# Layer 0's scores, sums, values and gate products in float32r, with the 16-token tile stacked by parts, and pairs of layer 1's small matmuls issued together

## The chip, the cores and the metric

The kernel runs on one core of a Trainium2 chip. The metric is device time of one execution in microseconds (us). The kernel before takes 1430.6 us, the median of three runs (1430.48 to 1431.33).

Five engines work in parallel and each executes its own instructions in order: TensorE (PE in the profile; its weight loads are listed apart as PEld), VectorE (DVE), ScalarE (ACT), GpSimd (POOL) and SyncE (SP), which here only issues DMAs.

## What is computed

The reference runs 272 tokens (16 learned meta tokens and 256 frames; the padding slots ahead of them are never computed) of width 2048 through two residual layers. Cut to what matters here:

```python
# layer 0: _even_mixer, one projection feeds both kinds of heads
log_a = log_sigmoid(gu @ w_gate2 + b_gate) / 16            # GLA gate, rank 16
scores = einsum('bcthk,bcshk->bchts', q_dec, k_inv)        # GLA, causal
o_intra = einsum('bchts,bcshv->bcthv', scores, v)
z = einsum('bhqd,bhkd->bhqk', qb, k)                       # stick-breaking, 8 heads of 128
ls = where(mask, log_sigmoid(-z), 0.0)
within = einsum('bhqnk,kl->bhqnl', ls, later_in_block)     # sums over later keys
w = where(mask, exp(log_sigmoid(z) + log_between), 0.0)
out = einsum('bhqk,bhkd->bhqd', w, v)
# layer 1: _odd_mixer, Mamba-2 SSD, 8 groups of 8 heads
y_diag = einsum('bctsgh,bcsghp->bctghp', l_mat * cb[..., None], xdt)
```

Each mixer is followed by an output projection, a residual add and a layer norm. Everything is float32. The kernel computes a float32 product either as a float32 matmul, or as three float32r matmuls on parts: an operand is split into a rounded high part and the rest, and hi·hi, lo·hi and hi·lo are accumulated.

## The kernel before

All 272 tokens are kept transposed, as columns; features lie on the 128 partitions. The program is a fixed list of units (`L0`, `L1`), each with one 128x2048 weight slice of 1 MB that SP loads into one of three buffers, that ACT rounds (`whi`, L146) and that DVE subtracts to get the rest (`wlo`, L147; in layer 1 POOL takes some). An input unit is 16 blocks of three float32r matmuls (`three`, L165 to L167) of a 128x128 weight block against 272 token columns; output units of layer 1 have 512 columns (L453 to L455). These are called the main stream below.

Between the blocks of a unit `tick()` advances a list of generators, which hold everything else: gates, scores, transposes, values, norms. `finish()` makes a unit wait in program order for the mixers that it needs. The order within each engine is then set by the framework's list scheduler, which works on the program's order, priorities and its own costs; so small matmuls end up as clusters between two matmuls of the main stream.

The tokens make three tiles: 0 to 127, 128 to 255 and the last 16. With attention causal, scores for the keys of the first tile need 272 query columns, those of the second 144, those of the last 16. In a layer-0 head the kernel before has:

- GLA gate (`gate_gla`, L494): a float32 matmul of `wg2` against `guT`, whose 128 rows hold four partial sums of the 16 rows of `gu`.
- Values to token order (`to_tokens`): PE transposes of `vraw`; the first token tile is split into `v0h`/`v0l`, the other two (`vt1`, `vt2`) stay float32.
- GLA values (`mix_gla`, L643 to L647): three float32r matmuls of 272 columns, one float32 of 144 columns, one float32 of 16 rows and 16 columns, for each of four value blocks.
- Stick-breaking (`mix_sb`): scores L705 to L707 in float32; the sums over later keys L724/L725 in float32r for the first tile and L726 to L730 in float32 for the others; values L742 to L746 as in GLA.

In layer 1, `x_path` transposes two feature blocks at a time (L1053, L1054) and `mix_ssd` computes 64-column pairs of heads with six float32 matmuls for each of four blocks j (L1100, L1102, L1104). PSUM has four `pj` buffers for the main stream, two `po` buffers for the small work and two `z` banks.

## Time and profile before

| | us |
|---|---|
| median of three runs | 1430.6 |
| the profiled execution | 1430.63 |
| its span, first to last instruction | 1428.9 |
| PE busy | 1408.6 |
| DVE busy | 980.7 |
| ACT busy | 762.7 |
| POOL busy | 334.0 |

The profiled execution is an ordinary one: it lies 0.03 us from the median, and 1.7 us of it lie outside the span. Matmul durations in a profile overlap, since PE is pipelined: three main matmuls of 0.29 us each start 0.12 us apart. What a matmul costs is therefore read here from the starts of a timeline (the time to the next start), not from durations. A float32 matmul of the program appears in the trace as two MATMULs and two LDWEIGHTS (so "x2" is one product); a float32r matmul and a transpose appear as one. The profile's names for shapes are rows*columns of the weight block, then the moving operand; all are printed as f32.

### The profile page before, as it was taken

The numbers are of one execution on the slowest core, as the hardware profiler recorded it, in microseconds if no ns is written. First come the engines' busy times: TensorE is split into PE (matmuls) and PEld (weight loads), VectorE is DVE, ScalarE is ACT, GpSimd is POOL, SyncE is SP. The second block draws the span as 40 slices with busy tenths as digits, with TensorE's granted clock in tenths as the row PEclk, the third lists the DMA queues.
The fourth block names the chain that finished last, engine by engine and source line by source line (L and its number), as shares of the span: only waits on it lengthen the run. The fifth ranks groups of instructions, "written<-read, shape, count | busy, mean of one in ns | idle before, by whom it ended". The sixth has DMA issues, their size and how long they took to land. (4 is left out here: it accounts for less than half of the span.)

```text
span 1428.9 us, 26055 instructions
## 1 busy us (share of the span) xinstructions
PE 1408.6 (99%) x10780; PEld 1337.7 (94%) x10780; DVE 980.7 (69%) x1522; ACT 762.7 (53%) x1133; POOL 334.0 (23%) x287
## 2 busy tenths in 40 slices
PE   9999999999999999999999999999999999999996
PEld 8999999999999999999999999899898998989985
DVE  6746574575565465447799989576876767767677
ACT  6545454354344544445587656565555555555651
POOL 0000100100101010004401535343432433434323
PEclk9999999999999999999999999999999999999998
DMA  8545444445454445444435554564554555445651
GB/s 318 181 151 173 153 153 172 167 159 177 148 178 148 148 148 192 148 148 144 150 132 216 193 199 166 207 225 167 206 178 166 207 181 220 153 172 179 207 207 59
DMA packets 37719, 249.83 MB, mean 175 GB/s; under 512 B 4256, under 2 KB 6112, under 8 KB 9184
## 3 DMA queue, kind: packets, MB, share of 16 engines
q1 hardware_dynamic: 37168, 247.77, 49.5%
q8 instruction: 84, 1.38, 0.4%
q10 hardware_dynamic: 432, 0.39, 0.1%
q14 instruction: 35, 0.29, 0.1%
HBM read 245.94 MB, written 2.20 MB: 174 GB/s over the span
## 5 line engine op out<-in xcount | busy, mean ns | idle before, releaser
L165 PE MATMUL pj<-xhi,whi 128*128 128x272 f32 (+4 forms) x2560 | 733.7, 287 | 1.8 <-DVE fix L845 1.5
L166 PE MATMUL pj<-xlo,whi 128*128 128x272 f32 (+4 forms) x2560 | 731.1, 286 | 0.1
L167 PE MATMUL pj<-xhi,wlo 128*128 128x272 f32 (+4 forms) x2560 | 730.2, 286 | 0.0
L147 DVE TENSOR_TENSOR wlo<-raw,whi 128x1024 fp32r<-128x1024 f32 (+2 forms) x405 | 508.9, 1260 | 280.7 <-ACT whi L146 278.3
L146 ACT ACTIVATE whi<-raw 128x1024 fp32r<-128x1024 f32 (+2 forms) x435 | 451.1, 1039 | 393.0 <-PE pj L166 324.8
L165 PEld LDWEIGHTS pj<-xhi,whi 128*128 128x128 f32 x2560 | 481.6, 188 | 5.1 <-DVE fix L845 1.9
L166 PEld LDWEIGHTS pj<-xlo,whi 128*128 128x128 f32 x2560 | 482.3, 188 | 2.1 <-issue 0.6
L167 PEld LDWEIGHTS pj<-xhi,wlo 128*128 128x128 f32 x2560 | 481.7, 188 | 0.5
L165 PE MATMUL pj<-mixh,whi 128*128 128x272 f32 x384 | 111.6, 292 | 0.0
L166 PE MATMUL pj<-mixl,whi 128*128 128x272 f32 x384 | 110.5, 288 | 0.0
L167 PE MATMUL pj<-mixh,wlo 128*128 128x272 f32 x384 | 110.2, 287 | 0.0
L147 POOL TENSOR_TENSOR wlo<-raw,whi 128x1024 fp32r<-128x1024 f32 x30 | 75.6, 2521 | 134.7 <-ACT whi L146 129.5
L453 PE MATMUL pj<-whi,yh 128*128 128x512 f32 (+1 forms) x244 | 97.3, 399 | 0.0
L454 PE MATMUL pj<-wlo,yh 128*128 128x512 f32 (+1 forms) x244 | 94.9, 389 | 0.0
L455 PE MATMUL pj<-whi,yl 128*128 128x512 f32 (+1 forms) x244 | 94.3, 386 | 0.0
L248 POOL TENSOR_TENSOR gr<-gr,gsc 128x1088 f32<-128x1088 f32 x6 | 15.4, 2572 | 307.0 <-ACT gsc L247 307.0
L165 PEld LDWEIGHTS pj<-mixh,whi 128*128 128x128 f32 x384 | 72.1, 188 | 0.5
L166 PEld LDWEIGHTS pj<-mixl,whi 128*128 128x128 f32 x384 | 72.3, 188 | 0.3
L167 PEld LDWEIGHTS pj<-mixh,wlo 128*128 128x128 f32 x384 | 72.3, 188 | 0.1
L462 DVE SCALAR_TENSOR_TENSOR acc<-pj,rr,acc 128x512 f32<-128x512 f32 (+1 forms) x65 | 47.4, 737 | 28.3 <-PE pj L455 28.2
L1108 POOL TENSOR_TENSOR yu<-yu,gz 128x256 f32<-128x256 f32 x32 | 44.9, 1408 | 82.2 <-DVE yu L1107 79.1
L455 PEld LDWEIGHTS pj<-whi,yl 128*128 128x128 f32 x244 | 45.9, 188 | 9.8
(309 smaller groups left out, 1497.8 us busy)
## 6 DMA issues: line engine op xcount, KB each, us to landing
raw<-in_wts SPq DMA_DIRECT2D x212, 1024.0 KB, 4.8
ebc<-edr SPq DMA_DIRECT2D x8, 1664.0 KB, 6.5
raw<-in_wts SPq DMA_DIRECT2D x9, 256.0 KB, 5.4
hacc<-in_xT SPq DMA_DIRECT2D x7, 272.0 KB, 5.4
early<-in_wts SPq DMA_DIRECT2D x2, 512.0 KB, 7.5
lg<-in_lnr SPq DMA_DIRECT2D x1, 1024.0 KB, 4.6
lb<-in_lnr SPq DMA_DIRECT2D x1, 1024.0 KB, 5.9
out_h<-acc SPq DMA_DIRECT2D x2, 512.0 KB, 2.6
```

The source lines that it names most:

```text
L146: self.nc.scalar.activation(hi, src, AF.Copy)
L147: eng.tensor_tensor(lo, src, hi.bitcast(F32), op=ALU.subtract)
L165: mm(ps, whi, xhi, start=first, stop=False)
L166: mm(ps, whi, xlo, start=False, stop=False)
L167: mm(ps, wlo, xhi, start=False, stop=last)
L248: mul(c, c, e, op=ALU.mult)
L453: mm(ps, yh[:, kk, tt], hi[:, k, :], start=kk == 0, stop=False)
L454: mm(ps, yh[:, kk, tt], lo[:, k, :], start=False, stop=False)
L455: mm(ps, yl[:, kk, tt], hi[:, k, :], start=False, stop=kk == 3)
L462: self.nc.vector.scalar_tensor_tensor(a, ps, r[:, t : t + 1], a, op0=ALU.mult, op1=ALU.add)
L1108: nc.gpsimd.tensor_tensor(u, u, z[:, j, :], op=ALU.mult)
```

## The change

In layer 0:

- Values of all three token tiles are float32r parts. `to_tokens` now handles two value blocks at a time and fills `vh`, `vl` for both 128-token tiles. The last 16 tokens are stacked by parts along the rows in `v2` (rows 0 to 15 hi, 32 to 47 lo, 64 to 79 hi) and meet `s2` with its parts stacked as hi, hi, lo: one float32r matmul with 80 rows gives all three products. `values` then issues three matmuls of 272 columns, three of 144 and one of 16 instead of the five above.
- Stick-breaking scores: q and k are split when they leave PSUM (`sb_parts`), and nine float32r matmuls replace three float32 ones. Sums: two of 272, two of 144 against `nL_r`, two of 144 against `nones_r`, and the last tile stacked in 48 rows (`sp2`, `nL2`) in two small matmuls.
- `parts_of` splits all 432 columns instead of 272 and copies the 16-token parts into the stack on DVE.
- Gate products: `add4`, one float32 matmul, sums the four partial sums of `gu`; `guS` (96 rows: hi, hi, lo) against `wg2r` (hi, lo, hi) is one float32r matmul. `wg2` has one buffer instead of two. The new constants are built at the start on DVE and POOL.

In layer 1 `x_path` emits all four blocks' transposes of a group together (the 16-row ones into a `z` bank), and `mix_ssd` emits the matmuls of two blocks j together. The units, their order, the weights and their DMAs stay.

```diff
--- before.py
+++ after.py
@@ -285,20 +285,32 @@
-        self.nones, self.nL, self.nL_r = [lp.tile([P, P], d, tag=n, name=n) for n, d in (("nones", F32), ("nL", F32), ("nL_r", F32R))]
+        self.nones_r, self.nL_r = [lp.tile([P, P], F32R, tag=n, name=n) for n in ("nones", "nL")]
+        nones, nL = [lp.tile([P, T], F32, tag="gs2", name=n, bufs=2)[:, :P] for n in ("nones_f", "nL_f")]
...
-        self.sel = lp.tile([P, P], F32, tag="sel", name="sel")
+        v2 = [lp.tile([80, 512], F32R, tag=f"v2{i}", name=f"v2{i}") for i in range(2)]
+        s2 = [lp.tile([80, 1, 16], F32R, tag=f"s2{i}", name=f"s2{i}") for i in range(2)]
+        self.v2, self.s2 = v2, s2
+        self.sp2, self.nL2 = [lp.tile([48, n, 16], F32R, tag=t, name=t) for n, t in ((2, "sp2"), (1, "nL2"))]
+        add4 = lp.tile([P, 432], F32, tag="ge", name="add4")[:, :P]
         for q in range(4):
-            nc.gpsimd.memset(self.sel[32 * q : 32 * q + 1, :], 1.0)
+            for r in range(4):
+                vec.tensor_copy(add4[32 * q : 32 * q + 32, 32 * r : 32 * r + 32], self.ident[32 * q : 32 * q + 32, 32 * q : 32 * q + 32])
...
@@ -335,7 +347,18 @@
         vec.tensor_copy(self.guT, ps[NS][:, :T])
-        vec.tensor_copy(self.nL_r, self.nL)
+        gs = self.po()
+        nc.tensor.matmul(gs[:, :T], add4, self.guT, start=True, stop=True)
+        act(self.guS[:64], gs[:64, :T], AF.Copy)
+        vec.tensor_tensor(self.guS[64:96], gs[:32, :T], self.guS[:32].bitcast(F32), op=ALU.subtract)
...
+        for a in v2 + [a.rearrange("p a b -> p (a b)") for a in s2 + [self.sp2, self.nL2]]:
+            vec.tensor_scalar(a, nones[: a.shape[0], 0:1].broadcast_to(a.shape), 0.0, None, op0=ALU.mult)
+        for q in (0, 32):
+            vec.tensor_copy(self.nL2[q : q + 16, 0, :], nL[:16, :16])
...
-            self.wg2 = self.lp.tile([P, 256], F32, tag="wg2", name=self.nm("wg2"), bufs=2)
+            self.wg2 = self.lp.tile([P, 256], F32, tag="wg2", name=self.nm("wg2"))
...
-        nc.tensor.matmul(ps[:, :T], self.sel, self.guT, start=True, stop=True)
+        nc.tensor.matmul(ps[:, :T], self.selx, self.guS, start=True, stop=True)
@@ -486,12 +509,15 @@
-        wg2 = self.wg2
+        wg2 = lp.tile([96, 256], F32R, tag="wg2r", name=self.nm("wg2r"))
+        act(wg2, self.wg2[:96], AF.Copy)
+        vec.tensor_tensor(wg2[32:64], self.wg2[:32], wg2[:32].bitcast(F32), op=ALU.subtract)
...
-            nc.tensor.matmul(ps[:, :T], wg2[:, j * P : (j + 1) * P], self.guT, start=True, stop=True)
+            nc.tensor.matmul(ps[:, :T], wg2[:, j * P : (j + 1) * P], self.guS, start=True, stop=True)
@@ -520,42 +546,66 @@
-    def parts_of(self, src):
-    def to_tokens(self, ps, v0h, v0l, vt1, vt2, j):
+    def parts_of(self, src, stack=None, rows=()):
+        n = src.shape[-1]
+        p = [self.lp.tile([P, 432], F32R, tag=t, name=self.nm(t), bufs=2)[:, :n] for t in ("s0h", "s0l")]
+        self.nc.scalar.activation(p[0], src, AF.Copy)
+        self.nc.vector.tensor_tensor(p[1], src, p[0].bitcast(F32), op=ALU.subtract)
+        for i, r in enumerate(rows):
+            a = stack[32 * i : 32 * i + 16]
+            b = p[r][:16, 0:16].rearrange("p (a b) -> p a b", a=1).broadcast_to([16, a.shape[1], 16])
+            self.nc.vector.tensor_copy(a, b)
+        return p
+    def to_tokens(self, raws, vh, vl, v2, j):
...
+        yield
+        pts = [self.po() for _ in raws]
+        for i, raw in enumerate(raws):
+            for t in range(2):
+                nc.tensor.transpose(pts[i][:, t * P : (t + 1) * P], raw[:, t * P : (t + 1) * P], self.ident)
+            nc.tensor.transpose(pts[0][:16, 256 + i * P : 256 + (i + 1) * P], raw[:, 256:272], self.ident)
...
+        w = slice(j * P, (j + len(raws)) * P)
+        t2 = pts[0][:16, 256 : 256 + len(raws) * P]
+        nc.scalar.activation(v2[:16, w], t2, AF.Copy)
+        for i, pt in enumerate(pts):
+            c = slice((j + i) * P, (j + i + 1) * P)
+            p = pt[:, : 2 * P].rearrange("p (t c) -> p t c", t=2)
+            nc.scalar.activation(vh[:, :, c], p, AF.Copy)
+            nc.vector.tensor_tensor(vl[:, :, c], p, vh[:, :, c].bitcast(F32), op=ALU.subtract)
+        nc.vector.tensor_tensor(v2[32:48, w], t2, v2[:16, w].bitcast(F32), op=ALU.subtract)
+        nc.vector.tensor_copy(v2[64:80, w], v2[:16, w])
...
+    def values(self, o, vh, vl, v2, c, sh, sl, s2):
+        mm = lambda r, a, b, start=False, stop=False: self.nc.tensor.matmul(
+            o[:, r], a, b, start=start, stop=stop, skip_group_check=True
+        )
+        for t, r, w in ((0, slice(0, T), slice(16, 288)), (1, slice(128, T), slice(288, 432))):
+            mm(r, vh[:, t, c], sh[:, w], start=t == 0)
+            mm(r, vh[:, t, c], sl[:, w])
+            mm(r, vl[:, t, c], sh[:, w])
+        mm(slice(256, T), v2[:, c], s2[:, 0, :], stop=True)
...
-        self.tasks["v", h, j] = self.push(self.to_tokens(ps, *self.cur["v", h], j))
+        raw = lp.tile([P, T], F32, tag="vraw", name=self.nm("vraw"), bufs=2)
+        self.nc.scalar.activation(raw, ps[:, :T], AF.Copy)
+        if j % 2:
+            self.tasks["v", h, j] = self.push(self.to_tokens([self.vraw, raw], *self.cur["v", h], j - 1))
+        self.vraw = raw
@@ -633,18 +683,14 @@
-        sh, sl = self.parts_of(s[:, 16:288])
+        st = self.s2[h % 2]
+        sh, sl = self.parts_of(s, st, (0, 0, 1))
...
+            self.values(o, *v, slice(j * P, (j + 1) * P), sh, sl, st)
@@ -675,40 +721,43 @@
+    def sb_parts(self, ps, tag, scale):
+        p = self.lp.tile([P, 2, T], F32R, tag=tag, name=self.nm(tag))
+        self.nc.scalar.activation(p[:, 0, :], ps[:, :T], AF.Copy, scale=scale)
+        self.nc.vector.scalar_tensor_tensor(
+            p[:, 1, :], ps[:, :T], scale, p[:, 0, :].bitcast(F32), op0=ALU.mult, op1=ALU.subtract
+        )
+        return p
...
-        self.cur["q"] = q
+        self.cur["q"] = self.sb_parts(ps, ("qe", "gq")[h % 2], SDH ** -0.5)
-        self.nc.vector.tensor_copy(self.cur["k"], ps[:, :T])
+        self.cur["k"] = self.sb_parts(ps, ("ke", "gk")[h % 2], 1.0)
...
     def mix_sb(self, h, q, k, v, tv):
-        mm(zb[:, 16:288], k[:, 0:128], q, start=True, stop=False, **gk)
-        mm(zb[:, 288:432], k[:, 128:256], q[:, 128:T], start=False, stop=False, **gk)
-        mm(zb[:16, 0:16], k[:, 256:T], q[:, 256:T], start=False, stop=False, **gk)
+        for a, b in ((0, 0), (0, 1), (1, 0)):
+            mm(zb[:, 16:288], k[:, a, 0:128], q[:, b, :], start=a == b, stop=False, **gk)
+        for a, b in ((0, 0), (0, 1), (1, 0)):
+            mm(zb[:, 288:432], k[:, a, 128:256], q[:, b, 128:T], start=False, stop=False, **gk)
+        for a, b in ((0, 0), (0, 1), (1, 0)):
+            mm(zb[:16, 0:16], k[:, a, 256:T], q[:, b, 256:T], start=False, stop=False, **gk)
...
+        sp = e = lp.tile([P, 432], F32, tag="ge", name=self.nm("sbe"))
@@ -718,16 +767,19 @@
-        sph, spl = self.parts_of(sp[:, 16:288])
-        mm(zb[:, 16:288], self.nL_r, sph, start=False, stop=False, **gk)
-        mm(zb[:, 16:288], self.nL_r, spl, start=False, stop=False, **gk)
-        mm(zb[:, 144:288], self.nones, sp[:, 288:432], start=False, stop=False, **gk)
-        mm(zb[:, 288:432], self.nL, sp[:, 288:432], start=False, stop=False, **gk)
-        mm(zb[:, 272:288], self.nones[:16, :], sp[:16, 0:16], start=False, stop=False, **gk)
-        mm(zb[:, 416:432], self.nones[:16, :], sp[:16, 0:16], start=False, stop=False, **gk)
-        mm(zb[:16, 0:16], self.nL[:16, :16], sp[:16, 0:16], start=False, stop=True, **gk)
+        sph, spl = self.parts_of(sp, self.sp2, (0, 1))
+        for s in (sph, spl):
+            mm(zb[:, 16:288], self.nL_r, s[:, 16:288], start=False, stop=False, **gk)
+        for s in (sph, spl):
+            mm(zb[:, 288:432], self.nL_r, s[:, 288:432], start=False, stop=False, **gk)
+        for s in (sph, spl):
+            mm(zb[:, 144:288], self.nones_r, s[:, 288:432], start=False, stop=False, **gk)
+        last = zb[:, 144:432].rearrange("p (a c) -> p a c", a=2)[:, :, 128:144]
+        mm(last, self.nones_r[:48, :], self.sp2, start=False, stop=False, **gk)
+        mm(zb[:16, 0:16], self.nL2[:, 0, :], self.sp2[:, 0, :], start=False, stop=True, **gk)
...
+        self.values(o, *v, slice(0, P), wh, wl, s2)
@@ -1045,23 +1094,31 @@
+        if j == 0:
+            return
+        pts = [self.po(), self.po()]
+        p2 = self.zbank()
+        for pt, jj in zip(pts, (0, 2)):
+            for i in range(2):
+                for t in range(2):
+                    nc.tensor.transpose(
+                        pt[:, t * 256 + i * P : t * 256 + (i + 1) * P], xt[:, jj + i, t * P : (t + 1) * P], self.ident
+                    )
+        for i in range(4):
+            nc.tensor.transpose(p2[:16, i * P : (i + 1) * P], xt[:, i, 256:T], self.ident)
...
+        for pt, jj in zip(pts, (0, 2)):
+            h0 = g * HPG + 2 * jj
+            c = slice(jj * P, jj * P + 256)
+            for t in range(2):
+                d = bd(self.est[:, 1, t, h0 : h0 + 4]).broadcast_to([P, 4, 64])
+                vec.tensor_tensor(hv(xd[:, t, c]), hv(pt[:, t * 256 : (t + 1) * 256]), d, op=ALU.mult)
+        d = bd(self.est2[:, 1, g * HPG : (g + 1) * HPG]).broadcast_to([16, HPG, 64])
+        vec.tensor_tensor(hv(xd2[:, :]), hv(p2[:16, :]), d, op=ALU.mult)
@@ -1091,18 +1148,21 @@
-            o = self.po()
...
-                mm(r[i][:, 0:S], xd[:, 0, c[i]], M[:, h[i], 0:256], start=True, stop=False, **gk)
...
-            yield
+            if j % 2 == 0:
+                os = {jj: self.po() for jj in (j, j + 1)}
+                gk = dict(skip_group_check=True)
+                for jj, o in os.items():
...
+                        mm(r[i][:, 0:S], xd[:, 0, c[i]], M[:, h[i], 0:256], start=True, stop=False, **gk)
...
+                yield
+            o = os[j]
```

Three places in the programs, as they were built. First PE, at the sums of a stick-breaking head (`z` is the bank with the scores, `s0h`/`s0l` the parts, `sp` the stack); before:

```order
L166 MATMUL pj_5113<-xlo,whi_5028 128x272
L725 MATMUL z_65<-s0l_5106,nL_r 128x272
L726 MATMUL z_65<-ppad,nones 128x144
L727 MATMUL z_65<-ppad,nL 128x144
L728 MATMUL z_65<-ppad,nones 128x16
L729 MATMUL z_65<-ppad,nones 128x16
L730 MATMUL z_65<-ppad,nL 16x16
L167 MATMUL pj_5113<-xhi,wlo_5029 128x272
```

and with the change:

```order
L165 MATMUL pj_5201<-xhi,whi_5154 128x272
L774 MATMUL z_65<-s0l_5191,nL 128x272
L776 MATMUL z_65<-s0h_5190,nL 128x144
L776 MATMUL z_65<-s0l_5191,nL 128x144
L778 MATMUL z_65<-s0h_5190,nones 128x144
L778 MATMUL z_65<-s0l_5191,nones 128x144
L781 MATMUL z_65<-sp_151,nones 128x2x16
L782 MATMUL z_65<-sp_151,nL_152 16x16
L166 MATMUL pj_5201<-xlo,whi_5154 128x272
```

One float32 product of 144 columns each for `nones` and `nL` has become two float32r ones, and the three products with the 16-token tile have become two with 48 rows. The cluster stands, as before, between two matmuls of the main stream.

Second PE, in `mix_ssd` of a late group (`M` is the decay matrix, `xd` the tokens-first x); before:

```order
L455 MATMUL pj_13229<-whi_13169,yl_11375 128x512
L1100 MATMUL po_13255<-M_12684,xd_12729 64x256 x2
L1102 MATMUL po_13255<-M_12684,xd_12729 64x144 x2
L1104 MATMUL po_13255<-mt,xd_1616_12730 64x16 x2
L453 MATMUL pj_13228<-whi_13197,yh_11374 128x512
L454 MATMUL pj_13228<-wlo_13198,yh_11374 128x512
L455 MATMUL pj_13228<-whi_13197,yl_11375 128x512
```

and with the change:

```order
L478 MATMUL pj_12480<-whi_12420,yl_10632 128x512
L1159 MATMUL po_12506<-M_11938,xd_11983 64x256 x2
L1161 MATMUL po_12506<-M_11938,xd_11983 64x144 x2
L1163 MATMUL po_12506<-mt,xd_1474_11984 64x16 x2
L1159 MATMUL po_12507<-M_11938,xd_11983 64x256 x2
L1161 MATMUL po_12507<-M_11938,xd_11983 64x144 x2
L1163 MATMUL po_12507<-mt,xd_1474_11984 64x16 x2
L476 MATMUL pj_12479<-whi_12448,yh_10631 128x512
```

Two blocks' matmuls now follow each other with no main matmul between them. This holds for fifteen of the sixteen pairs; in the first group the before kernel already has one such pair, and the first pair of the changed one is cut in two. The transposes of `x_path` are written together too, but in the built program each group still has two separate clusters of four 128-token and two 16-token transposes.

Third DVE, at the very start (`xlo` is the low part of the first tokens); before:

```order
L223 CAST ones_r<-ones 128x128
L338 CAST nL_r<-nL 128x128
L306 TENSOR_TENSOR xlo<-hacc,xhi 128x272
L147 TENSOR_TENSOR wlo_161<-raw_106,whi_160 128x256
L306 TENSOR_TENSOR xlo<-hacc,xhi 128x272
```

and with the change:

```order
L223 CAST ones_r<-ones 128x128
L356 CAST nones<-nones_f 128x128
L359 TENSOR_SCALAR v_147<-nones_f 80x512
L359 TENSOR_SCALAR v_148<-nones_f 80x512
L359 TENSOR_SCALAR s_149<-nones_f 80x16
L311 COPY add_153<-ident 32x32 x16
L355 CAST selx<-selx_f 96x128
L357 CAST nL<-nL_f 128x128
L359 TENSOR_SCALAR s_150<-nones_f 80x16
L359 TENSOR_SCALAR sp_151<-nones_f 48x32
L359 TENSOR_SCALAR nL_152<-nones_f 48x16
L318 TENSOR_TENSOR xlo<-hacc,xhi 128x272
```

The zeroing of the stacks and the sixteen copies that build `add4` now stand ahead of the first `xlo`.

More of the change, by code (lines that the diff above doesn't have):

```diff
@@ L617, in mix_gla @@
         q, k = self.cur["q", h], self.cur["k", h]
[L618 removed]
+        v = self.cur["v", h]
         g = self.cur["r", h]
[L620 removed]
+        yield from _wait(self.tasks["r", h], *[self.tasks["v", h, j] for j in (1, 3)])
         zb = self.zbank()
```

116 lines of the change are left out of this document (35 added, 81 removed).

## The prediction, made before the changed kernel was run

> **What bounds the kernel now.** I read the page first, then busy time by stretches (start:end and length in us, then busy us and instructions of PE, PEld, DVE, ACT, POOL, granted clock, DMA share, GB/s), then PE's waits.
>
> ```profile
> span 1428.9 us, 26055 instructions
> PE 1408.6 (99%) x10780; PEld 1337.7 (94%) x10780; DVE 980.7 (69%) x1522; ACT 762.7 (53%) x1133; POOL 334.0 (23%) x287
> ...
> 30.00:425.00 395.00, 395.00 (x3145) 389.84 (x3144) 243.95 (x398) 188.48 (x282) 26.25 (x28) 1.00 0.48 164
> 425.00:700.00 275.00, 275.00 (x2184) 269.74 (x2183) 157.56 (x203) 135.58 (x204) 49.43 (x77) 1.00 0.45 152
> 830.00:1417.00 587.00, 584.89 (x4237) 533.09 (x4236) 432.12 (x642) 324.98 (x457) 222.97 (x144) 1.00 0.52 183
> ...
> PE po L1053 <- POOL xt L955: 3.1, 5, 1.2
> ```
>
> From 30 to 700 us, layer 0, PE never stops, at the full granted clock; DVE is busy 60% of it and the DMA queues under half. In layer 1 the one wait of weight is 3.1 us for POOL ahead of the transposes. So a microsecond of PE time saved in layer 0 should be a microsecond of the end, as long as the other engines keep ahead. What each piece costs PE I read from starts on PE's timeline (start us, duration, line, tile, weights*shape, count).
>
> **The prices.** Ahead of each piece stands a main matmul, behind it another; from their starts I subtract the main stream's own 0.124 us each (601.20 − 601.08). Scores of one stick-breaking head:
>
> ```profile
> 601.08 0.29 PE L167 MATMUL pj<-xhi,wlo 128*128 128x272 f32 x1
> 601.20 0.62 PE L705 MATMUL z<-sqk 128*128 128x272 f32 x2
> 601.66 0.41 PE L706 MATMUL z<-sqk 128*128 128x144 f32 x2
> 602.00 0.21 PE L707 MATMUL z<-sqk 128*16 128x16 f32 x2
> ...
> 602.37 0.29 PE L166 MATMUL pj<-xlo,whi 128*128 128x272 f32 x1
> ```
>
> The piece costs 602.37 − 601.08 − 0.25 = 1.04 us. A float32 product of 272 columns takes 0.46, nearly four times the float32r 0.124. Sums of one head, with the values of one GLA block below them:
>
> ```profile
> 609.51 0.28 PE L166 MATMUL pj<-xlo,whi 128*128 128x272 f32 x1
> ...
> 609.76 0.41 PE L726 MATMUL z<-ppad,nones 128*128 128x144 f32 x2
> 610.00 0.41 PE L727 MATMUL z<-ppad,nL 128*128 128x144 f32 x2
> 610.34 0.39 PE L728 MATMUL z<-ppad,nones 16*128 16x16 f32 x2
> 610.58 0.37 PE L729 MATMUL z<-ppad,nones 16*128 16x16 f32 x2
> 610.88 0.21 PE L730 MATMUL z<-ppad,nL 16*16 16x16 f32 x2
> ...
> 611.25 0.29 PE L165 MATMUL pj<-xhi,whi 128*128 128x272 f32 x1
> ```
>
> ```profile
> 99.26 0.28 PE L165 MATMUL pj<-xhi,whi 128*128 128x272 f32 x1
> ...
> 99.76 0.41 PE L646 MATMUL po<-spad,gvt 128*128 128x144 f32 x2
> 100.09 0.39 PE L647 MATMUL po<-spad,gvt 16*128 16x16 f32 x2
> ...
> 100.64 0.29 PE L167 MATMUL pj<-xhi,wlo 128*128 128x272 f32 x1
> ```
>
> Sums: 611.25 − 609.51 − 0.25 = 1.49, and 0.13 for L724, which stands apart: 1.62. Values: 1.38 − 0.25 = 1.13. A float32 product of 144 columns takes 0.24 (609.76 to 610.00), and 0.34 where a matmul with fewer rows follows (610.00 to 610.34): 0.10 for the change of shape. L728 streams only 16 columns and yet takes 0.24, 0.12 for each of its two halves: below some 130 columns the load of 128 weight columns sets the pace.
>
> **The open price** is that of a float32r matmul of 144 columns; this trace has none under 256. Lower bound: its share of columns, 144/272 of 0.124 = 0.066. Upper bound: it is run as a float32 product, 0.24. I take 0.12, the weight load, because each of these matmuls loads 128 weight columns and L728 pays that with next to no columns. The small products of 16 columns I take at 0.03 to 0.07 with few weight columns (L730's two halves and the next load together take 0.14) and 0.12 with 128.
>
> The Trainium skill, "TensorE: Matmul & The Clock Gate", section "Back-to-back issue gap", gives about 81 ns per matmul of 128 columns in a sustained stream; by it the 120 new matmuls of 144 columns would cost some 4 us less than below. The same sentence has 131 ns for 512 columns, where this trace's main rows already have 124 ns for 272, so the trace does not bear it out.
>
> **Part by part.** Sum against the profiled execution's 1430.63 us, which is the median within 0.03.
>
> - Scores, 8 heads: 3 x 0.124 + 2 x 0.12 + 0.07 + 0.17 (three 16-column products and the next load) = 0.85 for 1.04: 1.5 us gained.
> - Sums, 8 heads: 0.25 + 4 x 0.12 + 0.15 (the two stacked products and the next load) = 0.88, and 0.17 for two changes of shape, since 48 rows are again fewer than 128: 1.05 for 1.62, 4.6 us. Without that change of shape 1.4 us more.
> - Values, 16 GLA blocks and 8 heads (there L742 to L746 are the same five products): 0.375 + 3 x 0.12 + 0.12 = 0.855 for 1.13: 24 x 0.275 = 6.6 us. I count no change of shape for 80 rows; at 0.17 each it would take 4.1 us back.
> - Gate products:
>
> ```profile
> 30.40 0.29 PE L167 MATMUL pj<-xhi,wlo 128*128 128x272 f32 x1
> 30.53 0.62 PE L356 MATMUL po<-guT,sel 128*128 128x272 f32 x2
> 30.98 0.62 PE L494 MATMUL po<-guT,wg 128*128 128x272 f32 x2
> ...
> 31.57 0.29 PE L166 MATMUL pj<-xlo,whi 128*128 128x272 f32 x1
> ```
>
> L356 and eight L494 cost 0.46 each; nine float32r at 0.125 and one new float32 (`add4`) replace them: 9 x 0.335 − 0.46 = 2.55 us.
> - Layer 1's pairs. One block, and two blocks that already stand together in group 0:
>
> ```profile
> 1261.36 0.39 PE L454 MATMUL pj<-wlo,yh 128*128 128x512 f32 x1
> 1261.58 0.39 PE L455 MATMUL pj<-whi,yl 128*128 128x512 f32 x1
> 1261.90 0.65 PE L1100 MATMUL po<-M,xd 128*64 128x256 f32 x4
> ...
> 1262.95 0.50 PE L453 MATMUL pj<-whi,yh 128*128 128x512 f32 x1
> 1263.29 0.40 PE L454 MATMUL pj<-wlo,yh 128*128 128x512 f32 x1
> ```
>
> ```profile
> 804.32 0.28 PE L166 MATMUL pj<-xlo,whi 128*128 128x272 f32 x1
> 804.53 0.65 PE L1100 MATMUL po<-M,xd 128*64 128x256 f32 x4
> ...
> 805.58 0.65 PE L1100 MATMUL po<-M,xd 128*64 128x256 f32 x4
> ...
> 806.86 0.29 PE L165 MATMUL pj<-xhi,whi 128*128 128x272 f32 x1
> ```
>
> Main matmuls of 512 columns start 0.22 to 0.23 apart (1261.58 − 1261.36). Alone: 1263.29 − 1261.58 = 1.71, less two of them, 0.45: 1.26. Together: 2.54 − 0.25 = 2.29. So 0.23 a pair; 14 new pairs: 3.2 us. The second block's matmuls now fill the other `po` buffer, so the next pair waits until DVE has read both; the built order has 18 main matmuls (4 us) between pairs, and I cost it at nothing.
> - Transposes: in the built order the clusters of `x_path` stay two per group, and most of `to_tokens` stay single. Fewer alternations of 128 and 16 columns: 0.5 us (0 to 1). POOL's 3.1 us stay; the first cluster stands later, the second earlier.
> - The start loses. DVE sits idle 1.84 us ahead of its first `xlo`; about 3 us now go in front of it: two zeroings of 512 columns, some 0.5 each, and sixteen copies, 0.07 apart if they go like the small copies below, plus a few casts.
>
> ```profile
> 4.39 0.44 DVE L306 TENSOR_TENSOR xlo<-hacc,xhi 128x272 fp32r<-128x272 f32 x1 [1.84 <-ACT xhi L305]
> ...
> 714.70 0.15 DVE L844 COPY uv<-po 64x2 f32<-64x2 f32 x1
> 714.77 0.14 DVE L844 COPY uv<-pj 128x2 f32<-128x2 f32 x1
> ...
> L590 DVE SCALAR_TENSOR_TENSOR gq<-pj,qe 128x16 f32<-128x16 f32 x8 | 1.3, 165 | 0.0
> ```
>
> PE's L166 waits behind it; I take 1.0 us (0.3 to 2.2, the last if a copy takes L590's 0.165).
> - DVE's added work in layer 0 is costed at nothing, hidden by the 40% of DVE that is idle: per stick-breaking head one more split from PSUM (0.44), two splits of 432 instead of 272 columns, five stack copies (0.165 each) and a wider value split, together about 1.9 us; per GLA head about 2.1. Eight and four of them: 23 us over 670 us. Uncovered it costs up to these 23 us. SP's `wg2` loads now wait for ACT and DVE to read the one buffer, with weight loads queued behind; three buffered units of 6 us each cover that.
>
> Sum: 1.5 + 4.6 + 6.6 + 2.55 + 3.2 + 0.5 − 1.0 = 17.95 us. 1430.63 − 17.95 = **1412.7 us**.
>
> **The rivals.**
>
> *B: under 256 columns float32r is no faster than float32.* For it: the kernel has not one such matmul today. Against it: nothing in the rows from 256 to 512 columns hints at a step. With 0.24 for each 144-column matmul the scores become 1.27 (1.8 us lost), the sums 1.53 (0.7 gained), the values 1.215 (2.0 lost); with the rest, 2.2 us are left: 1428.4. The skill's "FP8 and Floating Point Precision", "TensorE Precision Notes", has true FP32 as four passes and the reduced form as a read truncated to FP22, with no limit on columns; that speaks against B, and the 0.46 against 0.124 above agrees with four passes to one.
>
> *C: slower, through DVE.* The place is DVE's queue in layer 0: splits of weights (L147) stand behind the added copies, PE's next block behind the split. If all of the added 23 us reached PE, 1412.7 + 23 = 1436. It decides from the point where more than 18 of them do. Against it: PE today waits for no split from 30 to 700 us.
>
> *D: cheaper still.* Weight loads overlap, 144 columns cost 0.066 and the stack pays no change of shape: 120 x 0.054 + 1.4 = 7.9 us more: 1404.8.
>
> **How the numbers follow.** Forecast 0.68 (own range 1408 to 1418: the start, 80 and 96 rows, transposes), D 0.12, B 0.14, C 0.06. The range 1404 to 1422 leaves out B and C, 0.20. What can be told from no change is about 0.2%, 2.9 us: the forecast and D are faster (0.80); B lies at the edge, 0.03 faster, 0.09 the same, 0.02 slower; C 0.01 the same, 0.05 slower. So 0.83, 0.10, 0.07.
>
> **What would show it.** On PE's timeline: float32r matmuls of 144 columns 0.12 apart (B: 0.24, D: 0.07); a head's sums near 1.05 us, scores and values near 0.85; gates at 0.125; pairs in layer 1 near 2.3. PE still without waits from 30 to 700 us; if not, the wait names DVE and C is right. DVE's first `xlo` near 5.5 us. The forecast is wrong if PE's time per piece falls and the span does not.

## The result, and the profile after

The changed kernel takes **1409.91 us** (median of 4 runs, 1409.64 to 1410.04) where the kernel before took 1430.54 (4 runs, 1430.23 to 1431.33): ratio 0.9855, 95% interval 0.9838 to 0.9872. That is 20.6 us faster; 1412.7 was forecast, in a range of 1404 to 1422. The profiled execution took 1410.01 us, span 1408.3 against 1428.9.

Busy time by stretches of the changed kernel (same columns as in the prediction):

```profile
30.00:425.00 395.00, 395.00 (x3199) 393.24 (x3198) 255.28 (x417) 194.79 (x283) 29.73 (x29) 1.00 0.49 167
425.00:700.00 275.00, 272.50 (x2205) 269.67 (x2204) 176.54 (x269) 141.89 (x223) 51.58 (x77) 1.00 0.46 158
...
830.00:1396.50 566.50, 566.50 (x4107) 520.94 (x4108) 419.39 (x614) 315.20 (x441) 209.92 (x142) 1.00 0.52 183
```

PE still never stops from 30 to 425 us, at the full clock; DVE went from 244 to 255 us of these 395 and has room left. The second row now reaches past layer 0's norm (at 689 us, before at 703) and holds its waits; the third ends, like the one before, 12 us ahead of the end. PE's waits after (who waits and for whom: us in total, times, longest):

```profile
PE pj L165 <- ACT mixh L801: 1.0, 1, 1.0
...
PE po L1105 <- POOL xt L1004: 0.3, 1, 0.3
```

The 3.1 us for POOL's `xt` at the transposes fell to 0.3, and a wait of 1.0 us for ACT's `mixh` is new.

One head's sums on PE's timeline (start us, duration, line, tile, weights*shape, count):

```profile
446.13 0.29 PE L165 MATMUL pj<-xhi,whi 128*128 128x272 f32 x1
...
446.38 0.23 PE L776 MATMUL z<-s0h,nL 128*128 128x144 f32 x1
446.45 0.28 PE L776 MATMUL z<-s0l,nL 128*128 128x144 f32 x1
446.56 0.27 PE L778 MATMUL z<-s0h,nones 128*128 128x144 f32 x1
446.68 0.27 PE L778 MATMUL z<-s0l,nones 128*128 128x144 f32 x1
446.88 0.28 PE L781 MATMUL z<-sp,nones 48*128 48x32 f32 x1
447.01 0.17 PE L782 MATMUL z<-sp,nL 48*16 48x16 f32 x1
447.11 0.40 PE L166 MATMUL pj<-xlo,whi 128*128 128x272 f32 x1
447.34 0.29 PE L167 MATMUL pj<-xhi,wlo 128*128 128x272 f32 x1
```

447.34 − 446.13 − 2 x 0.124 = 0.96, and 0.13 for the first product, which stands apart: 1.10 for 1.62 before. Of the 144-column products the first costs 0.07 and each further one 0.11; ahead of the product on 48 rows stand 0.20. The last products of a block of values, with the weight loads (PEld) between them:

```profile
452.80 0.23 PE L590 MATMUL po<-s0h,gvh 128*128 128x144 f32 x1
452.80 0.19 PEld L590 LDWEIGHTS po<-s0l,gvh 128*128 128x128 f32 x1
452.87 0.27 PE L590 MATMUL po<-s0l,gvh 128*128 128x144 f32 x1
452.91 0.19 PEld L590 LDWEIGHTS po<-s0h,gvl 128*128 128x128 f32 x1
452.98 0.28 PE L590 MATMUL po<-s0h,gvl 128*128 128x144 f32 x1
453.02 0.19 PEld L590 LDWEIGHTS po<-s,v 80*128 80x128 f32 x1
453.09 0.22 PE L590 MATMUL po<-s,v 80*128 80x16 f32 x1
453.16 0.37 PE L166 MATMUL pj<-xlo,whi 128*128 128x272 f32 x1
```

Loads start no closer than 0.11 us (452.80, 452.91, 453.02), and the products follow them. On 80 rows nothing stands ahead of the stack.

The ledger over the whole trace: for every piece between main matmuls, the time from the main matmul ahead to the fourth one behind (fewer where the next piece comes sooner), less the main stream's own spacing, summed by kind. The 9,660 main matmuls are the same in both.

| us on PE | before | after | gained | forecast |
|---|---|---|---|---|
| scores (8) | 8.41 | 6.64 | 1.77 | 1.5 |
| sums (8) | 13.00 | 8.81 | 4.19 | 4.6 |
| values (24) | 27.42 | 20.99 | 6.43 | 6.6 |
| gate products | 4.16 | 1.62 | 2.54 | 2.55 |
| layer 1's M products (32 blocks) | 40.08 | 37.65 | 2.43 | 3.2 |
| x transposes | 15.69 | 11.22 | 4.47 | 0.5, with the next row |
| token transposes, norms | 9.06 | 9.07 | 0.0 | |
| layer 1's `cb` and sums of squares | 13.01 | 11.78 | 1.23 | 0 |
| start: to the first main matmul, and delays to 13 us | 6.83 | 7.61 | −0.78 | −1.0 |
| delays in the main stream after 13 us | 2.49 | 3.88 | −1.39 | 0 |
| behind the last matmul's start | 11.42 | 11.71 | −0.29 | 0 |

With 0.03 in pieces that the change leaves alone this is 20.6 us.

### The profile page after: what moved, and what is told of

Its sections match the earlier page's. It is cut to its first block, busy times and chain, and to the rows that moved or that the text cites. A ratio compares the mean times of both kernels' runs of the same rounds, so it can differ in the third digit from the quotient of the medians.

```text
span 1408.3 us, 26132 instructions
## 1 busy us (share of the span) xinstructions
PE 1390.1 (99%) x10765; PEld 1332.7 (95%) x10765; DVE 1003.8 (71%) x1613; ACT 769.3 (55%) x1138; POOL 320.9 (23%) x285
## 4 chain that ended last, share of the span: by engine, by line
PE 89%; DVE 6%; ACT 2%; issue 1%; DMA 1%; POOL 0%; ACTq 0%; SPq 0%; DVEq 0%; POOLq 0%
PE pj L165 23%; PE pj L166 23%; PE pj L167 23%; PE pj L476 4%; PE pj L478 4%; PE pj L477 4%; DVE wlo L147 2%; PE po L1159 1%; PE po L590 1%; ACT whi L146 1%; DVE xlo L816 1%; PE po L1161 1%; PE po L1163 0%; ACT hacc L923 0%; DMA ebc<-edr 0%
## 5 line engine op out<-in xcount | busy, mean ns | idle before, releaser
L166 PE MATMUL pj<-xlo,whi 128*128 128x272 f32 (+4 forms) x2560 | 731.7, 286 | 0.2 <-DVE xlo L318 0.2
L166 PEld LDWEIGHTS pj<-xlo,whi 128*128 128x128 f32 x2560 | 483.0, 189 | 1.8 <-issue 0.6
L166 PE MATMUL pj<-mixl,whi 128*128 128x272 f32 x384 | 110.4, 288 | 0.0
L166 PEld LDWEIGHTS pj<-mixl,whi 128*128 128x128 f32 x384 | 72.3, 188 | 0.2
L476 PEld LDWEIGHTS pj<-whi,yh 128*128 128x128 f32 x244 | 45.8, 188 | 9.0
```

What stands on the lines that cost most here:

```text
L166: mm(ps, whi, xlo, start=False, stop=False)
L476: mm(ps, yh[:, kk, tt], hi[:, k, :], start=kk == 0, stop=False)
```

## The experiments

Two theories at the start. **A**: the surplus over the forecast comes from layer 1's merges themselves, because the transposes no longer wait for POOL. **Rival**: the waits vanished because layer 0 now ends at another moment. Beside it stood the prices of the stack and of the small products, the start, and how much DVE work fits.

### The two halves apart, and x_path alone

E1 is the kernel before with `x_path` and `mix_ssd` of the change, E2 the changed kernel with these two as before. `mix_ssd` in E1:

```diff
-            o = self.po()
...
+            if j % 2 == 0:
+                os = {jj: self.po() for jj in (j, j + 1)}
...
+            o = os[j]
```

> The kernel before with only the merged clusters of layer 1 (x_path and mix_ssd of the change); layer 0 as before. Theory A (layer 1's part of the gain, 6.8 us between the end of layer 0 and the end of the span by the starts on PE, comes from the merges themselves: 3.2 us for 14 pairs, the rest because PE no longer waits for POOL at the transposes): 1430.5 - 6.8 = 1423.7 us, and PE's wait at the transposes for xt falls from 3.1 us to under 1. Rival (the waits for POOL vanished because layer 0 now hands over at another moment; the merges bring the pairs alone, as I predicted): 1430.5 - 3.2 = 1427.3 us, waits near 3 us.

> The changed kernel with x_path and mix_ssd of the kernel before: layer 0's changes alone. Theory A: 1409.9 + 6.8 = 1416.7 us, with waits for POOL's xt near 3 us again. Rival: 1409.9 + 3.2 = 1413.1 us, waits under 1. If the two parts are independent, this run's gain and that of the other half add up to 20.6 us.

E1: 1424.85 us, ratio 0.9957 (0.9940 to 0.9973), 6.1 us below the 1430.98 of the kernel before on the same chip. E2: 1415.25, ratio 0.9891 (0.9877 to 0.9906), 15.7 us below. Together 21.8 for 20.6: nearly independent. In E1 the transposes cost 10.69 us on PE and no wait for `xt` is left; in E2 they cost 14.57 and `PE po L1102 <- POOL xt L1004` stands at 2.3 us. Both times lie between the two forecasts, nearer to A's (off by 1.2 and 1.5 of the 3.6 us between them), and the waits go as A has it. Why shows in one group of the kernel before and of the changed one (POOL's row first, then PE's):

```profile
1060.20 1.37 POOL L955 TENSOR_TENSOR xt<-xt,xcl 128x544 f32<-128x544 f32 x1 [1.25 <-ACT xcl L954]
...
1061.26 0.28 PE L167 MATMUL pj<-xhi,wlo 128*128 128x256 f32 x1
1061.62 0.44 PE L1053 MATMUL po<-ident,xt 128*128 128x128 f32 x2
```

```profile
1042.02 1.38 POOL L1004 TENSOR_TENSOR xt<-xt,xcl 128x544 f32<-128x544 f32 x1 [1.26 <-ACT xcl L1003]
...
1047.16 0.28 PE L167 MATMUL pj<-xhi,wlo 128*128 128x256 f32 x1
1047.28 0.60 PE L1105 MATMUL po<-ident,xt 128*128 128x128 f32 x4
```

Before, the group's first cluster stood right behind POOL's multiplication (1061.57, then 1061.62), 0.24 us late. That is one of the mild cases: of the five waits that make up the 3.1 us, four, 2.8 us together, stand at the first cluster of a group, the longest 1.2 us. After, the first cluster belongs to the task of the second pair of tiles and comes, in this group, 3.9 us behind POOL's end.

E11 takes `x_path` alone into the kernel before:

```diff
-        pt = self.po()
-        p2 = self.po()
...
+        if j == 0:
+            return
+
+        pts = [self.po(), self.po()]
+        p2 = self.zbank()
...
```

> The kernel before with x_path of the change alone: both clusters of transposes of a group in the later task; mix_ssd as before. If the gain beyond the pairs comes from here (the first cluster of a group stood right behind POOL's multiplication, 1061.62 behind 1060.20 + 1.37; it now stands some 4 us later): transposes fall from 15.7 to 10.7 us on PE's starts, 5.0 us, of which about 1 to 2 may be given back elsewhere, 1426 to 1427.5 us, and no wait of PE for xt at the transposes in the groups after the second. If the gain needs the pairs as well (another order of the whole layer): waits near 3 us and 1430.5.

1428.98 us (10 runs, 1427.67 to 1430.86) against 1430.88 on the same chip, ratio 0.9986 (0.9977 to 0.9995): 1.9 us, a small gain but one that the interval leaves standing. It is neither of the two expectations: less than the 3.0 to 4.5 us of the first, more than the nothing of the second. The waits end as expected: transposes 11.08 us, and of the waits for `xt` 0.2 us are left. Of these 4.6 us and 1.2 at `cb` and the sums of squares, about 2 went back into the main stream of layer 1, the rest into the start, the M products and the end. So theory A's reason holds on PE's timeline and only in part in time: by subtraction, some 2 of E1's 6.1 us are `x_path`'s and 4 come with the pairs, which no run has alone.

### What the stacked products cost

E3 puts the stack of the sums on 80 rows, E4 the 16-token products of layer 1 on 128, with zeros in the new rows; PE's order is the same, instruction by instruction, but for four products of one pair in E4, at 788 us.

```diff
-        self.sp2, self.nL2 = [lp.tile([48, n, 16], F32R, tag=t, name=t) for n, t in ((2, "sp2"), (1, "nL2"))]
+        self.sp2, self.nL2 = [lp.tile([80, n, 16], F32R, tag=t, name=t) for n, t in ((2, "sp2"), (1, "nL2"))]
...
-        mm(last, self.nones_r[:48, :], self.sp2, start=False, stop=False, **gk)
+        mm(last, self.nones_r[:80, :], self.sp2, start=False, stop=False, **gk)
```

> The changed kernel with the stack of the stick-breaking sums on 80 rows, zeros in the new ones, in place of 48: the same matmuls in the same order. If a product on fewer than about half of the rows costs 0.09 us on entering and as much on leaving, as I put into the sum (0.17), the sums of one head fall from 0.97 us to about 0.79 and the time by 8 x 0.18 = 1.4 us to 1408.5. If the 0.20 us ahead of the stacked product belongs to something else (the two runs of 16 columns that it writes, the wait for the products before it), nothing changes: 1409.9.

E3 took 1409.35 us (1408.10 to 1410.08), ratio 0.9849 (0.9834 to 0.9864). The median gains some 0.6, less than expected and no more than two measurements of the changed kernel differ (E10, below), but the piece itself gained more, 8.81 to 6.76 us. The end of one head's sums:

```profile
446.46 0.27 PE L778 MATMUL z<-s0l,nones 128*128 128x144 f32 x1
446.57 0.23 PE L781 MATMUL z<-sp,nones 80*128 80x32 f32 x1
446.65 0.17 PE L782 MATMUL z<-sp,nL 80*16 80x16 f32 x1
446.67 0.37 PE L166 MATMUL pj<-xlo,whi 128*128 128x272 f32 x1
446.88 0.29 PE L167 MATMUL pj<-xhi,wlo 128*128 128x272 f32 x1
```

From L778's last to the second main matmul 0.42 us, where the changed kernel has 0.66 (446.68 to 447.34). The stretch from the first scores to the end of layer 0, before its norm, is 2.0 us shorter (249.5 for 251.5). In this profile the rest went: `norm0` 1.0 us longer, `xt` 0.7, delays of the main stream 0.8. The norm's 1.0 is not the edit's: the granted clock was 0.50 there, from 687.6 to 691.0 us, and so it was in E10, the changed kernel itself, from 689.7 to 693.1, with the same longer norm.

```diff
-        self.mt = lp.tile([16, HPG, 16], F32, tag="mt", name="mt")
+        self.mt = lp.tile([P, HPG, 16], F32, tag="mt", name="mt")
+        self.xd2 = lp.tile([P, 512], F32, tag="xd2", name="xd2")
+        self.nc.gpsimd.memset(self.mt, 0.0)
+        self.nc.gpsimd.memset(self.xd2, 0.0)
```

> The changed kernel with the 16-token products of layer 1 (xd2 and mt) on 128 rows, zeros in the new ones, in place of 16; the zeros are written once at the start of layer 1; the same matmuls in the same order. If fewer rows cost on entering and leaving: 0.10 us (216 ns against 116) on entering each of 32 blocks and up to as much on leaving: 3.2 to 6.4 us, so 1403.5 to 1406.7, and a pair falls from 2.31 us to 1.9 to 2.1. If the 0.10 belongs to the 16 columns and not to the rows: 1409.9, pairs at 2.31.

E4: 1404.01 us, ratio 0.9813 (0.9798 to 0.9828), 5.9 us below the changed kernel. Inside one pair, first the changed kernel, then E4:

```profile
1242.43 0.42 PE L1161 MATMUL po<-M,xd 128*64 128x144 f32 x4
1242.78 0.29 PE L1163 MATMUL po<-mt,xd 16*64 16x16 f32 x4
1243.00 0.65 PE L1159 MATMUL po<-M,xd 128*64 128x256 f32 x4
```

```profile
1238.22 0.41 PE L1164 MATMUL po<-M,xd 128*64 128x144 f32 x4
1238.46 0.24 PE L1166 MATMUL po<-mt,xd 128*64 128x16 f32 x4
1238.55 0.63 PE L1162 MATMUL po<-M,xd 128*64 128x256 f32 x4
```

Entering the product on 16 rows costs 0.11 (0.35 for 0.24), leaving it 0.13 (0.22 for 0.09); a pair fell from 2.31 to 1.91 us. It is the rows, since columns and order did not change, and a wait is not what vanished. This agrees with the Trainium skill, "TensorEngine Tiling (Array Packing)", section "Key Properties", by which a change of tiling mode drains TensorE; it gives no price, and the runs here give 0.1 us each way.

E7 widens the three 144-column value products of each block to 256 columns.

```diff
-        for t, r, w in ((0, slice(0, T), slice(16, 288)), (1, slice(128, T), slice(288, 432))):
+        for t, r, w in ((0, slice(0, T), slice(16, 288)), (1, slice(16, T), slice(176, 432))):
```

> The changed kernel with the three 144-column value products of each block widened to 256 columns (more columns of the scores tile are added to more output columns, so the values of columns 16 to 128 are no longer the reference's). If the load of 128 weight columns sets their pace, the first of three goes from 0.067 to 0.114 us and the others stay at 0.11: 24 x 0.055 = 1.3 us more, 1411.2. If columns set it, the others go from 0.11 to 0.19: 24 x 0.22 = 5.3 us more, 1415.2.

```profile
453.43 0.28 PE L590 MATMUL po<-s0h,gvh 128*128 128x256 f32 x1
453.56 0.28 PE L590 MATMUL po<-s0l,gvh 128*128 128x256 f32 x1
453.67 0.28 PE L590 MATMUL po<-s0h,gvl 128*128 128x256 f32 x1
453.79 0.17 PE L590 MATMUL po<-s,v 80*128 80x16 f32 x1
453.81 0.37 PE L166 MATMUL pj<-xlo,whi 128*128 128x272 f32 x1
```

The wide products start 0.11 to 0.13 apart, the stack behind them now 0.02 ahead of the main matmul, and all values cost 21.45 us for 20.99: 0.02 a block, less even than the load theory's 0.055, because what the first product loses the stack gets back. Columns do not set the pace up to 256. The run as a whole took 1413.06 us, 3.1 more than the changed kernel, not through the values: its built order of layer 1 had moved, with 0.5 us more at the transposes and 2.0 more of delays in the main stream, 1.1 of them in the waits for `fix` after layer 0's norm.

E6 issues the six value products as 272, 144, 272, 144, 272, 144 columns.

```diff
-            mm(r, vh[:, t, c], sh[:, w], start=t == 0)
-            mm(r, vh[:, t, c], sl[:, w])
-            mm(r, vl[:, t, c], sh[:, w])
+        for v, sx in ((vh, sh), (vh, sl), (vl, sh)):
+            for t, r, w in parts:
+                mm(r, v[:, t, c], sx[:, w], start=v is vh and sx is sh and t == 0)
```

> The changed kernel with the six value products in another order: 272 and 144 columns in turn, in place of three and three. If the weight loads set the pace of the 144-column products (loads never start less than 0.11 us apart, and a 272-column product leaves 0.124), a load of the short ones now falls under a long one and a block costs 0.02 to 0.04 us less: 24 blocks, 0.5 to 1.0 us, so 1408.9 to 1409.4, and the starts of the short products lie 0.06 to 0.09 behind the next. If each 144-column product costs 0.11 by itself, whatever stands beside it, nothing changes: 1409.9 and 0.11 after each.

1409.66 us (1409.51 to 1411.53), ratio 0.9852 (0.9835 to 0.9868); values 21.12 us for 20.99. Nothing gained: the expectation of 0.02 to 0.04 a block was wrong. But the sign that it named came true. Two pairs of one block, each of the first two rows a 272-column product with the 144-column one behind it, and then the stack:

```profile
452.28 0.35 PE L590 MATMUL po<-s0l,gvh 128*128 128x272 f32 x2
452.47 0.40 PE L590 MATMUL po<-s0h,gvl 128*128 128x272 f32 x2
452.70 0.22 PE L590 MATMUL po<-s,v 80*128 80x16 f32 x1
```

In the whole trace 71 of the 72 products of 144 columns start 0.065 to 0.072 us ahead of the next matmul, so a fixed 0.11 for each is out. The 272-column matmul behind such a product then takes 0.17 in place of 0.124, and what the short one saved is gone: the two take 0.24 together, and loads still start no closer than 0.11.

### The start

E5 moves the sixteen copies of `add4` to POOL and makes the zeroings from a tile that is written late:

```diff
-                vec.tensor_copy(add4[32 * q : 32 * q + 32, 32 * r : 32 * r + 32], self.ident[32 * q : 32 * q + 32, 32 * q : 32 * q + 32])
+                nc.gpsimd.tensor_copy(add4[32 * q : 32 * q + 32, 32 * r : 32 * r + 32], self.ident[32 * q : 32 * q + 32, 32 * q : 32 * q + 32])
...
-            vec.tensor_scalar(a, nones[: a.shape[0], 0:1].broadcast_to(a.shape), 0.0, None, op0=ALU.mult)
+            vec.tensor_scalar(a, self.guT[: a.shape[0], 0:1].broadcast_to(a.shape), 0.0, None, op0=ALU.mult)
```

> The changed kernel with the sixteen copies for add4 on POOL and the zeroings made from a tile that is written only at 26 us, so that DVE has about 0.5 us of small casts ahead of its first xlo in place of 3.2. If those 3.2 us delay PE at the start as I put it (1.0 us), first xlo goes from 5.35 to about 4.4 us and the time to 1409.9 - 0.8 = 1409.1. Rival: the start is set by the arrival of hacc and by PE's own warm-up matmuls, since the run with layer 1's merges alone began its main stream at 5.36 us too, with nothing new on DVE: 1409.9 within 0.5.

1414.07 us, ratio 0.9884 (0.9869 to 0.9898): slower than the changed kernel by 4.2, which neither theory had. The start itself settles the question. PE in E5, then in the kernel before:

```profile
3.58 2.13 PE L227 MATMUL po<-ones 128*128 128x128 f32 x9
5.36 0.57 PE L165 MATMUL pj<-xhi,whi 128*128 128x272 f32 x1
```

```profile
3.58 1.60 PE L227 MATMUL po<-ones 128*128 128x128 f32 x9
4.93 0.37 PE L165 MATMUL pj<-xhi,whi 128*128 128x272 f32 x1
```

DVE's first `xlo` came at 4.53 in E5, not 5.35, and the first main matmul still at 5.36, behind warm-up matmuls that took longer than in the one profile of before. E1 and E11, whose layer 0 is the old one, also begin at 5.36. Delays to 13 us were 1.82 in E5, 2.25 and 2.06 in two profiles of the changed kernel, 2.63 and 2.21 in E1 and E11. DVE's 3.2 us cost PE 0.4 at most, within the scatter. The longer warm-up goes with the clock: the trace's record of it begins, at full clock, at 4.5 us in the profile of before and between 4.9 and 7.3 in all the others, with DVE's new work (5.7 and 7.0 in two profiles of the changed kernel) and without it (6.4 in E1, 5.7 in E11, 6.8 in E5). Until then matmuls run slower: E1's second and third main matmul start 0.22 and 0.23 us ahead of the next.

The 4.2 us were lost in layer 1. The edit moved the built order there: the second cluster of transposes stands at 771.2 us, 5.3 behind the first, where the changed kernel has 19.1 between them. PE's wait, POOL's row and DVE's rows:

```profile
PE po L1105 <- POOL xt L1004: 3.9, 2, 2.8
```

```profile
769.49 4.76 POOL L1004 TENSOR_TENSOR xt<-xt,xcl 128x544 f32<-128x544 f32 x1 [5.61 <-ACT xcl L1003]
...
769.79 1.21 DVE L147 TENSOR_TENSOR wlo<-raw,whi 128x1024 fp32r<-128x1024 f32 x1
770.93 0.97 DVE L1068 TENSOR_TENSOR M<-M,cb 128x800 f32<-128x800 f32 x1
771.83 1.21 DVE L147 TENSOR_TENSOR wlo<-raw,whi 128x1024 fp32r<-128x1024 f32 x1
```

POOL's multiplication, 1.4 to 2.5 us in the changed kernel, took 4.76: it began as DVE started three operations of two inputs in SBUF in a row, and ended 1.2 us after the last of them (773.04). The next one took 4.58 and ended 1.2 us after such a row, too. Behind PE's wait of 2.8 us the granted clock was 0.50 from 774.8 to 778.2 us, which is part of the loss. The Trainium skill, "SBUF — State Buffer", section "Who interferes with whom", has one port pair shared by the two engines under an exclusive lock; the rows agree. That DVE's next instruction takes the lock again ahead of POOL is how I read the rows; no run tested it.

### DVE's added work

E12 issues the split in `parts_of` three times in place of once, E8 nine times.

```diff
-        self.nc.vector.tensor_tensor(p[1], src, p[0].bitcast(F32), op=ALU.subtract)
+        for _ in range(3):
+            self.nc.vector.tensor_tensor(p[1], src, p[0].bitcast(F32), op=ALU.subtract)
```

> The changed kernel with DVE's split in parts_of issued three times in place of once: 2 x (20 x 0.607 + 4 x 0.44) = 27.8 us more of DVE in layer 0, about what the change itself adds. The ninefold split cost 30 us of its 111, some 22 of them in layer 0, most of that in products that waited for their own ninth split, and 5 in layer 1, where the built order had moved. If cover ends somewhere above the 23 us that the change adds, this one costs under 2 us in layer 0 (up to 5 more if the order in layer 1 moves too): 1410 to 1412, or up to 1417 with the moved order. If each added microsecond costs a fifth from the first on (22 of 111): 5.6 us in layer 0.

> The changed kernel with DVE's split in parts_of (the subtraction alone) issued nine times in place of once: 8 x (20 x 0.607 + 4 x 0.44) = 111 us more of DVE in layer 0, nearly five times what I counted the change to add. My theory: DVE is idle for some 240 us of layer 0, so this is hidden, with at most 3 us of waits: 1410 to 1413. Theory C (DVE's added work reaches PE, because the splits of weights stand behind it): with the 23 us of the change nothing showed, so its threshold lies higher; from there on each microsecond counts, and up to 111 us come on top: 1440 to 1520.

E12: 1414.98 us, 4.5 above the changed kernel on the same chip (E10, below). E8: 1439.99. From the first scores to layer 0's norm: 251.5 us in the changed kernel, 254.2 in E12, 276.9 in E8. In the GLA part (30 to 425 us) PE has no wait in either, with DVE at 282 of 395 us in E8. So most of the added work is hidden, as my theory had it, but its bound of 3 us did not hold for E8: 25 us were lost between the first scores and the norm. Most of them stand in three waits, and not for a split of weights, as theory C has it, but for the heads' own split:

```profile
PE po L591 <- DVE s0l L556: 16.0, 3, 9.1
```

All of PE's waits in that stretch are 19 us in E8 and 2.5 in the changed kernel. Much of what is left of the 25 goes with the clock: the granted clock was 0.50 from 550.0 to 556.8 and from 655.8 to 679.7 us, around these waits, and a main matmul took 0.227 there in place of 0.124; at 0.10 more for each of the 77 matmuls that start there, an estimate is 8 us. So E8 prices waits and what follows them, not DVE's microseconds alone.

E12's 2.7 us there are a little over the 2 that were expected and half of the 5.6 of the other reading; the rest of its 4.5 came later, 1.1 of it at the sums of squares and 1.1 in the waits for `fix`. The loss in layer 0 stands at one place, the last head, where nothing is left to cover its chain:

```profile
649.83 0.40 PE L591 MATMUL po<-s0l,gvh 128*128 128x272 f32 x1 [1.78 <-DVE s0l L556]
...
651.69 1.04 PE L165 MATMUL pj<-mixh,whi 128*128 128x272 f32 x4 [0.99 <-ACT mixh L802]
```

The first is DVE's added work reaching PE. The second is in the changed kernel too, the 1.0 us for `mixh` at 649.88, and in E2, and not in the kernel before: there, main matmuls that need no new `mixh` follow the last values, and in the changed kernel's built order none are left. Whether the head's longer chain on DVE and ACT has put the values so late in that order is not shown; in the trace of the changed kernel DVE was done with the last copy at 646.92, 1.2 us before PE took it up. Behind the two waits of E12 the granted clock (the third number from the end) falls, too, from 1.00 to:

```profile
652.00:654.00 2.00, 2.00 (x11) 2.00 (x10) 0.87 (x3) 0.55 (x1) 0.28 (x1) 0.50 0.00 0
```

### Both paddings, and the changed kernel beside them

E9 has the edits of E3 and E4, E10 is the changed kernel.

> The changed kernel with both paddings: the sums' stack on 80 rows and layer 1's 16-token products on 128 rows. If the two add up: on PE's starts 2.05 us from the sums (8.81 to 6.76 in the run with the first alone) and 6.4 + 0.4 us from the pairs (39.3 to 32.5 in the run with the second alone); of the first 0.6 us of the median arrived and of the second 5.9. So 1409.9 - 5.9 - 0.6 to 2.05 = 1402.0 to 1403.4 us. Rival: shorter sums only bring PE sooner to the next wait, as the run on 80 rows alone seemed to show (2.05 us less in the sums, more in waits elsewhere): 1404.0, as with the second padding alone.

> The changed kernel itself, beside the others on the same chip, so that differences under 1 us can be told: 1409.9 us within 0.5. If it stands lower by 0.5 or more, the gain of the 80 rows alone (1409.35) is less than it looked; if higher, more.

E9: **1402.19 us** (1401.99 to 1404.31), ratio 0.9799 (0.9786 to 0.9812); E10: 1410.50 (1409.25 to 1411.22), ratio 0.9853 (0.9840 to 0.9867). The two add up: sums 6.75, M products 30.85 us for 37.65, together 8.9 on PE, of which 8.3 arrive. E9 is the fastest of all, 28.7 us below the 1430.88 of the kernel before on that chip. E10 stands 0.6 above the first measurement, so differences of that size between two measurements say nothing.

## Why the prediction was right, point by point

- **What bounds the kernel.** Right: a microsecond off PE in layer 0 is a microsecond of the end. Layer 0's four items gained 14.9 us on PE, and E2, with them alone, 15.7.
- **The open price.** Taken at 0.12, measured 0.07 for the first 144-column product of a run and 0.11 for the others, set by the load, as E6 and E7 show. Rival B (0.24) is out. Rival D's 0.066 holds only for a product behind a longer one, the first of a run.
- **Scores, sums, values, gates.** 0.83, 1.10, 0.83 and 0.13 us where 0.85, 1.05, 0.855 and 0.125 were taken. The 0.17 for entering and leaving 48 rows was low: E3 gives 2.05 / 8 = 0.26. Nothing for 80 rows: right. The values gained 7.6 us, 0.32 a block and more than forecast, and lost 1.1 of it at the last head.
- **DVE's added work at nothing.** Right but for the last head, where PE now waits 1.0 us for `mixh`; how much of that is DVE's added work stays open. Rival C is out: with five times the added work PE waited for the heads' own splits, and still for no split of weights.
- **The pairs.** 0.23 a pair, right: the 14 new pairs went from 35.55 to 32.27 us, 3.28. The four blocks of group 0 cost 0.85 more, which was not in the sum. No pair waits for DVE's reading of `po`.
- **The transposes.** The step that failed: "POOL's 3.1 us stay; the first cluster stands later, the second earlier." The movement was right, but 2.8 of the 3.1 us of waits were the first cluster's, so moving it later ended them: with the fewer alternations 4.5 us, and 1.2 more at `cb` and the sums of squares, where 0.5 stood in the sum.
- **The start.** The other failed step: "PE's L166 waits behind it; I take 1.0 us." The profiles differ by 0.8, the number is near, and the mechanism is not shown: without DVE's work the start (first main matmul and delays) took 8.0 us in E1, 7.6 in E11 and 7.2 in E5, with it 7.6 and 7.4 in two profiles, and 6.8 in the one of before. At most 0.4 are DVE's, so the closeness is largely luck.
- **Not in the sum:** 1.4 us more of delays in the main stream. Most are a few nanoseconds at a time, between 256-column matmuls of layer 1: of 1438 gaps 1036 were under 116 ns before and 566 after, the others mostly 117 to 119. They go with the merges: E1 has 515 of 1442 under 116 ns, E2 1286 of 1442. Why is open: whole stretches between two clusters run at one pace or the other, behind clusters that waited and behind clusters that did not.

The time came out 2.8 us below the forecast, by the transposes (5.2 over) less the delays in the stream (1.4), the pairs (0.8) and small items. That the sum held is thus partly two errors of opposite sign.

## What to carry to other kernels

Price a small matmul by its weight load, not by its columns, until the columns outlast the load. Give it as many rows as its neighbours where zeros are cheap: here two paddings without one instruction less gave 8.3 us, four tenths of what the whole rewrite gave. When a static order is rebuilt, look in the new order at the distance between each producer and its consumer, and at the last link of each chain, which has no cover behind it.

## What the runs showed of the hardware that was not expected

- A change between full rows and few rows costs about 0.1 us in each direction (0.11 entering and 0.13 leaving 16 rows; 0.26 for both with 48), and nothing at 80 rows.
- A POOL operation of 1.4 to 2.5 us took 4.76 beside three DVE operations in a row.
- Short waits of PE can be followed by 3.4 us at a granted clock of 0.50: in E12 two within 4 us (1.8 and 1.0). The single wait of 1.0 in the changed kernel was not. Their length alone does not decide: the waits ahead of layer 0's norm (0.6, 0.2 and 0.7 us) were followed by it in E3, E6 and E10, and not in the first profiles of the two kernels or in E9. A difference of 1 us between two profiles can be this.
- Edits at the start of the program moved the built order of layer 1, 700 us later, and cost some 4 us there (E5). A run that undoes a part must be read by its trace as well as by its time.
